# A hybrid decoder trunk: x, p, the vectors and the output pass the host with channels first

## The chip, the cores and the metric

The kernel runs on one core of one Trainium2 chip. The metric is the device time of one execution in microseconds (us).

## The reference

Two residual layers over 2048 tokens of 1024 channels, then a final norm, all in fp32. Cut to what matters:

```python
h = x
for i in range(2):
    hn = rmsnorm(h, norm_gain[i])        # h * rsqrt(mean(h*h over channels) + 1e-6) * gain
    if i == 0:                            # z = hn @ w_in, split in 8
        h = h + concat(retention(q, k, v) * silu(g), stick_breaking(q, k, v) * silu(g)) @ w_out
    else:                                 # RWKV-7 time mixing: six shifted mixes of hn, delta-rule recurrence
        h = h + (y * silu(g)) @ w_out
    gate = sigmoid(h @ ple_gate[i])
    h = h + gate * (p[i] @ ple_proj[i])   # p[i]: 2048 x 256
return rmsnorm(h, final_gain)
```

Every projection by weights takes its input with channels on the 128 partitions, since TensorE contracts over the partitions.

## The kernel before, in words

The tokens go in two halves of 1024 (`w` = 0 and 1), each half in two blocks of 512 (`TB`) or eight tiles of 128. Channels stand in 8 blocks of 128 (`NB`). An fp32 operand is kept as a high and a low fp32r part (`split`: a cast on ACT, a subtraction on DVE or POOL), and a product takes three matmuls (`mm3`, L258 to L260).

Stages, with their place in the profiled span:

- 0 to 300 us: `l0_norm(0)` and `retention(0)`. Eight tiles of x (128 tokens x 1024 channels) are loaded; Square with a sum on ACT gives their 1/rms; PE transposes each 128x128 block (`xp`, L419) into channels first. The result is written to `xT` in DRAM for the residual, and multiplied by gain and 1/rms (`hf`) and split into the activations `hn`. 1/rms is a column for each token tile; four matmuls of a broadcast column by the identity turn it into a row on all partitions (`rbp`, L390). The retention projects one head at a time.
- 300 to 530 us: `stick(0)`, the projections of the stick-breaking heads (each result split again and written to DRAM) and its attention.
- 530 to 740 us: `tail(0, 0)`: out projection, residual (`r`, L798, L799), gate, and the projection of p. p is loaded by tokens and transposed on PE (`pt`, L817). A generator, `next_stats(1)`, runs beside it: it transposes the second half of x (`nt`, L449), writes it to DRAM (`xnext`, L454) and computes its 1/rms.
- 740 to 1210 us: `l1_proj(0)`, the projections of layer 1.
- 1210 to 1910 us: the second half's `l0_norm_next`, `retention(1)` and `stick(1)`. Beside the stick-breaking attention layer 1's recurrence of the first half begins at 1714 us.
- 1910 to 2380 us: that recurrence beside `tail_lean`, which is the second half's tail of layer 0.
- 2380 to 2930 us: `l1_proj(1)`. 2930 to 3610 us: the second half's recurrence beside `tail_lean` of layer 1 for the first half and for block 0 of the second. `tail_lean` transposes p too (`pt`, L996).
- 3610 to 3786 us: `tail(1, 1)` for the last block, and beside it `finish`, which loads the other three blocks' results channels first (`fx`), transposes them on PE (`ft`, L911), scales them by 1/rms on ACT and writes them out by tokens. The last block's own results (32 blocks of 128x128) are transposed at L874, kept, and scaled when its 1/rms is there (L887, L889).

The Tile framework orders the instructions of each engine by its own schedule. DMAs issued on SP run in that order, and one that waits holds back those behind it.

Of the kernel before, what the change touches and what calls it, by code (L numbers as in the profile page):

```python
# [133 lines left out]
class Trunk:  # L134
    def __init__(self, ctx, tc, ins, out):
# [23 lines left out]
        self.rs_kept = self.cst.tile([P, NHALF * NTT], F32, name="rs_kept")  # L159
        self.dd, self.parts = {}, {}  # L160
# [17 lines left out]
    def load_vectors(self):  # L178
        nc, i = self.nc, self.i
        flat = lambda a: a.rearrange("(b p) -> b p", p=P)  # L180
        rows = [
            (V_G0, i["norm_gain"].rearrange("j (b p) -> (j b) p", p=P)),
            (V_GF, flat(i["final_gain"])),
            (V_W0, flat(i["rwkv_w0"][0])),
            (V_A0, flat(i["rwkv_a0"][0])),
            (V_KK, flat(i["rwkv_k_k"][0])),
            (V_KA, flat(i["rwkv_k_a"][0])),
            (V_RK, i["rwkv_r_k"][0].rearrange("(b h) n -> b (h n)", h=2)),
            (V_MU, i["odd_mu"][0].rearrange("j (b p) -> (j b) p", p=P)),
            (V_GN, flat(i["ret_gn_gain"][0])),  # L190
        ]
        n = V_N * NB
        v = self.cst.tile([P, n], F32, name="vec")
        with self.tc.tile_pool(name="vl", bufs=1) as vl, self.tc.tile_pool(name="vps", bufs=1, space=PSUM) as vps:
            t = vl.tile([n, P], F32, name="vrows")
            nc.gpsimd.memset(t, 0.0)
            for j, src in rows:
                nc.sync.dma_start(t[j * NB : j * NB + src.shape[0], :], src)
            yield
            ps = vps.tile([P, n], F32, name="vt")  # L200
            nc.tensor.transpose(ps, t, self.ident[:n, :n])
            nc.vector.tensor_copy(v, ps)
# [162 lines left out]
    def l0_norm(self, w):  # L365
        nc, tc = self.nc, self.tc
        self.hn = self.new_acts()
        self.xT = [self.dr.tile([P, HT], F32, name=self.u("xT")) for _ in range(NB)]
        with (
            tc.tile_pool(name="n0x", bufs=2, side="right") as sx,  # L370
            tc.tile_pool(name="n0", bufs=2, side="right") as sb,
            tc.tile_pool(name="n0p", bufs=1, space=PSUM, side="right") as psp,
        ):
            xs, st = [], sx.tile([P, NTT], F32, name="st", bufs=1)

            def load(t):
                xt = sx.tile([P, D], F32, tag="x", name=self.u("x"), bufs=NTT)
                r0 = w * HT + t * P
                nc.sync.dma_start(xt, self.i["x"][0, r0 : r0 + P, :])
                xs.append(xt)  # L380

            def stats(t):
                sq = sx.tile([P, D], BF16, tag="sq", name=self.u("sq"), bufs=1)
                nc.scalar.activation(sq, xs[t], AF.Square, accum_out=st[:, t : t + 1])

            def scales(tb):
                rs = self.rsqrt(sx, st[:, tb * 4 : tb * 4 + 4], 1.0 / D, RMS_EPS, 4, "rs")
                rbp = psp.tile([P, TB], F32, tag="rb", name=self.u("rbp"))
                for j in range(4):
                    nc.tensor.matmul(  # L390
                        rbp[:, j * P : (j + 1) * P],
                        rs[:, j : j + 1].to_broadcast([P, P]),
                        self.ident,
                        start=True,
                        stop=True,
                    )
                rb = sb.tile([P, TB], F32, tag="rbs", name=self.u("rb"))
                nc.scalar.copy(rb, rbp)
                return rb

            for t in range(4):
                load(t)
            if w == 0:
                vectors = self.load_vectors()
                next(vectors)
            for t in range(4):
                load(t + 4)
                stats(t)
            if w == 0:
                for _ in vectors:  # L410
                    pass
            for tb in range(NTB):
                rb = scales(tb)
                for d in range(NB):
                    if tb == 0 and d % 2:
                        stats(4 + d // 2)
                    xp = psp.tile([P, TB], F32, tag="xp", name=self.u("xp"), bufs=3)
                    for j in range(4):
                        nc.tensor.transpose(xp[:, j * P : (j + 1) * P], xs[tb * 4 + j][:, d * P : (d + 1) * P], self.ident)  # L419
                    xo = sb.tile([P, TB], F32, tag="xo", name=self.u("xo"))  # L420
                    nc.scalar.copy(xo, xp)
                    nc.sync.dma_start(self.xT[d][:, tb * TB : (tb + 1) * TB], xo)
                    hf = sb.tile([P, TB], F32, tag="hf", name=self.u("hf"))
                    nc.vector.scalar_tensor_tensor(hf, xp, self.col(V_G0, d), rb, op0=ALU.mult, op1=ALU.mult)
                    sl = slice(tb * TB, (tb + 1) * TB)
                    self.split(hf, self.hn[d][0][:, sl], self.hn[d][1][:, sl], nc.gpsimd if d % 2 else nc.vector)

    def next_stats(self, w, sb, pt):

        nc = self.nc  # L430
        self.xnext = self.dr.tile([P, NB, HT], F32, name=self.u("xT"))
        st = self.rs_kept.rearrange("p (q t) -> p q t", q=2)
        units, xs = [(t, q) for t in range(NTT) for q in range(2)], []

        def load(t, q):
            x = sb.tile([P, 4, P], F32, tag="nx", name=self.u("nx"))
            r0 = w * HT + t * P
            nc.sync.dma_start(x.rearrange("p a b -> p (a b)"), self.i["x"][0, r0 : r0 + P, q * TB : (q + 1) * TB])
            xs.append(x)

        load(*units[0])
        for n, (t, q) in enumerate(units):
            if n + 1 < len(units):
                load(*units[n + 1])
            yield
            x = xs.pop(0)
            tp = pt.tile([P, 4, P], F32, tag="pt", name=self.u("nt"))
            for j in range(4):
                nc.tensor.transpose(tp[:, j], x[:, j], self.ident)  # L449
# [1441 lines left out]
```

## Time and profile before

| what | value |
|---|---|
| three runs | 3775.52, 3779.46, 3786.1 us; median 3779.46 us |
| profiled execution, its own time | 3787.24 us |
| its span | 3785.5 us |
| mean granted TensorE clock | 0.943 of full speed |
| busy share of the span | PE 93%, DVE 52%, ACT 37%, POOL 26% |

The span runs from the first to the last instruction of the profiled execution; its own time is that execution's as the runs' times are taken. PE is matmul on TensorE, PEld its weight loads, DVE VectorE, ACT ScalarE, POOL GpSimd, SP the engine that issues most DMAs.

### The profile page before, as it was taken

What the parts mean: (1) busy time and instruction counts of PE and PEld (TensorE: products, weight loads), DVE (VectorE), ACT (ScalarE), POOL (GpSimd) and SP (SyncE); (2) the same over time, 40 slices, a digit from 0 to 9 for tenths busy, and PEclk for the clock granted to TensorE, in tenths of its full rate; (3) what the DMA queues carried; (4) which work ended last, traced back from release to release, by engine and by line L of the source; (5) the groups of instructions that cost most, each with busy time, mean ns of one, the idle gap of its engine ahead of it and who ended that gap; (6) DMA issues with size and microseconds to landing.
All of it is one profiled execution on the core that took longest, in us unless ns stands there. A gap on an engine that the chain in (4) does not pass through costs nothing.

```text
span 3785.5 us, 66193 instructions
## 1 busy us (share of the span) xinstructions
PE 3536.1 (93%) x25929; PEld 2801.1 (74%) x25929; DVE 1954.3 (52%) x3884; ACT 1412.1 (37%) x2767; POOL 986.2 (26%) x1036
## 2 busy tenths in 40 slices
PE   8999999899999999998979999899988799999978
PEld 6888877777666788887767777677656677777757
DVE  4334541453675433457956756542574477567532
ACT  5233453344553221445522322243553233223233
POOL 4345543400000222455512312200000143122322
PEclk9999999999999999999969999599989799989989
DMA  6348866655587225546456665343575876556485
GB/s 234 103 170 268 226 191 208 208 168 177 194 260 272 74 95 171 174 107 134 88 150 203 177 179 150 110 143 123 185 240 179 203 226 200 156 166 197 161 284 179
DMA packets 593792, 675.14 MB, mean 178 GB/s; under 512 B 215764, under 2 KB 443976, under 8 KB 562504
## 3 DMA queue, kind: packets, MB, share of 16 engines
q1 hardware_dynamic: 510056, 577.95, 49.3%
q10 hardware_dynamic: 42848, 59.39, 4.4%
q0 software_dynamic: 40576, 33.56, 4.2%
q8 instruction: 205, 3.36, 0.4%
q14 instruction: 107, 0.88, 0.1%
HBM read 414.78 MB, written 255.98 MB: 177 GB/s over the span
## 4 chain that ended last, share of the span: by engine, by line
PE 32%; DMA 8%; DVE 7%; SPq 3%; ACT 1%; issue 1%; POOL 1%; ACTq 0%; POOLq 0%; DVEq 0%
PE pj L258 6%; PE pj L259 6%; PE pj L260 6%; PE g L1490 2%; PE y L1652 2%; PE s L1630 1%; PE y L1649 1%; DMA wraw<-in_odd_w_out 1%; DMA w<-parts 1%; PE u L1593 1%; DMA g<-g 1%; DVE prd L1521 1%; PE x L1615 1%; PE kt L1603 1%; DVE wb L1527 1%
## 5 line engine op out<-in xcount | busy, mean ns | idle before, releaser
L258 PE MATMUL pj<-act,w 128*128 128x512 f32 x1216 | 498.5, 414 | 20.3 <-ACT act L218 9.8
L260 PE MATMUL pj<-act,w 128*128 128x512 f32 x1216 | 498.2, 410 | 4.0 <-POOL w L219 4.0
L259 PE MATMUL pj<-act,w 128*128 128x512 f32 x1216 | 496.6, 409 | 0.4 <-POOL act L219 0.4
L258 PE MATMUL pj<-xs,w 128*128 128x512 f32 x768 | 298.4, 403 | 18.1 <-DMA w<-parts 6.5
L259 PE MATMUL pj<-xs,w 128*128 128x512 f32 x768 | 307.0, 400 | 5.2 <-DVE xs L219 5.1
L260 PE MATMUL pj<-xs,w 128*128 128x512 f32 x768 | 302.4, 397 | 0.0
L258 PEld LDWEIGHTS pj<-act,w 128*128 128x128 f32 x1216 | 237.8, 196 | 72.0 <-ACT act L218 11.3
L260 PEld LDWEIGHTS pj<-act,w 128*128 128x128 f32 x1216 | 237.7, 195 | 56.4 <-POOL w L219 4.9
L259 PEld LDWEIGHTS pj<-act,w 128*128 128x128 f32 x1216 | 238.5, 196 | 50.5 <-POOL act L219 0.8
L258 PE MATMUL pj<-w,act 128*128 128x512 f32 x640 | 259.0, 408 | 10.8 <-ACT sg L535 7.1
L712 DVE TENSOR_TENSOR_SCAN rr<-om,rr,ones 128x512 f32<-128x512 f32 (+3 forms) x160 | 216.7, 1361 | 77.1 <-ACT om L706 68.6
L259 PE MATMUL pj<-w,act 128*128 128x512 f32 x640 | 254.9, 398 | 0.0
L260 PE MATMUL pj<-w,act 128*128 128x512 f32 x640 | 253.5, 399 | 0.0
L721 POOL TENSOR_TENSOR be<-be,rr 128x512 f32<-128x512 f32 (+3 forms) x160 | 167.3, 1048 | 192.6 <-DVE rr L712 87.2
L219 POOL TENSOR_TENSOR w<-wraw,w 128x1024 fp32r<-128x1024 f32 x72 | 159.4, 2218 | 173.4 <-ACT w L218 152.1
L258 PEld LDWEIGHTS pj<-xs,w 128*128 128x128 f32 x768 | 146.9, 192 | 67.2 <-issue 15.6
L1490 PE MATMUL g<-xr,kb 64*128 64x128 f32 x1024 | 149.7, 309 | 34.9 <-DVE grb L1498 20.6
L259 PEld LDWEIGHTS pj<-xs,w 128*128 128x128 f32 x768 | 146.9, 191 | 43.5 <-DVE xs L219 11.8
L260 PEld LDWEIGHTS pj<-xs,w 128*128 128x128 f32 x768 | 147.0, 192 | 34.3 <-issue 3.3
L1490 PEld LDWEIGHTS g<-xr,kb 64*128 64x128 f32 x1024 | 121.6, 203 | 60.0 <-DVE grb L1498 22.2
L258 PEld LDWEIGHTS pj<-w,act 128*128 128x128 f32 x640 | 121.9, 191 | 39.2 <-ACT sg L535 10.3
L218 ACT CAST w<-wraw 128x1024 fp32r<-128x1024 f32 x105 | 104.4, 1000 | 123.0 <-PE pj L260 27.2
(364 smaller groups left out, 7760.2 us busy)
## 6 DMA issues: line engine op xcount, KB each, us to landing
w<-parts SPq DMA_DIRECT2D x145, 1024.0 KB
parts<-w SPq DMA_DIRECT2D x97, 1024.0 KB
wraw<-in_odd_w_in SPq DMA_DIRECT2D x32, 512.0 KB
ar<-ar SPq DMA_DIRECT2D x32, 512.0 KB
w<-v SPq DMA_DIRECT2D x128, 128.0 KB
xr<-ar SPq DMA_DIRECT2D x64, 256.0 KB
kb<-kb SPq DMA_DIRECT2D x32, 512.0 KB
kg<-dk POOLq DMA_DIRECT2D x24, 512.0 KB, 5.0
```

The costliest lines, as they stand in the source:

```text
L218: nc.scalar.copy(hi, src)
L219: (lo_eng or nc.vector).tensor_tensor(lo, src, hi.bitcast(F32), op=ALU.subtract)
L258: nc.tensor.matmul(ps, a[0], b[0], start=first, stop=False)
L259: nc.tensor.matmul(ps, a[0], b[1], start=False, stop=False)
L260: nc.tensor.matmul(ps, a[1], b[0], start=False, stop=last)
L712: nc.vector.tensor_tensor_scan(rr[:, 0:kw][:, ::-1], om[:, ::-1], self.ones.to_broadcast([P, kw]), rr[:, kw : kw + 1], op0=ALU.mult, op1=A ...
L721: nc.gpsimd.tensor_tensor(be, be, rr[:, 1 : kw + 1], op=ALU.mult)
L1490: nc.tensor.matmul(ps[:, j], kb[br, 4 * g + j], xr[br, par, 4 * g + j], start=True, stop=True)
L1521: nc.vector.tensor_tensor(pr[:, :k, :n], nb[:, m, k:].unsqueeze(1).to_broadcast([P, k, n]), wb[:, :k, m:k].to_broadcast([P, k, n]), op=ALU ...
L1527: nc.vector.tensor_tensor(wb[:, :k, k:], wb[:, :k, k:], pr[:, :k, :n], op=ALU.add)
L1593: nc.tensor.matmul(ps[hs, ob], lhs[hs, ob], rhs[hs, ob], start=True, stop=True)
L1652: nc.tensor.matmul(o, d["grb"][hs, ob], uv[hs, par, ob], start=False, stop=True)
```

## The change

The host hands over x twice, as it was and transposed (`xT`, 1024 x 2048), p transposed (`pT`) and all vectors as one table (`vec`); the kernel's output is 1024 x 2048, and the host transposes it. What follows inside:

- `l0_norm`, `next_stats` and `l0_norm_next` are gone. `l0_in` loads 128x512 blocks of `xT` and multiplies them by the gain alone: the high part on ACT, the low part in one operation on DVE. These loads stand between the loads of the first head's weights.
- `l0_stats` loads x by tokens as well, two tiles at a time, and takes its squares. 1/rms stays as columns (`rs0`) and as rows in DRAM (`rb0`). It is applied to the results: in the retention as the scale of the operations that read PSUM, in the stick-breaking projections through one new DVE multiplication for each result, into a tile `f` that has one buffer (the gate's result is written to DRAM straight from it), and for `v` in the operations of its split.
- The tails load p by `pT`. In `finish` and at the end of `tail`, results are multiplied by 1/rms as rows on DVE and written channels first; the end's eight writes go to SP and ACT by turns.

The diff, cut to its core:

```diff
+    def l0_in(self, w, sb, tb, ds):
+
+        nc = self.nc
+        sl = slice(tb * TB, (tb + 1) * TB)
+        for d in ds:
+            x = sb.tile([P, TB], F32, tag="x", name=self.u("x"), bufs=8)
+            nc.sync.dma_start(x, self.xT[d][:, sl])
+            hi, lo = [a[:, sl] for a in self.hn[d]]
+            g = self.col(V_G0, d)
+            nc.scalar.activation(hi, x, AF.Copy, scale=g)
+            nc.vector.scalar_tensor_tensor(lo, x, g, hi.bitcast(F32), op0=ALU.mult, op1=ALU.subtract)
+
+    def l0_stats(self, w, sb, psp):
+
+        nc = self.nc
+        self.rb0 = self.dr.tile([P, HT], F32, name=self.u("rb0"))
+        st = sb.tile([P, NTT], F32, name=self.u("st"), tag="st", bufs=1)
+        for tb in range(NTB):
+            for t in range(4 * tb, 4 * tb + 4):
+                xt = sb.tile([P, D], F32, tag="xt", name=self.u("xt"))
...
+                sq = sb.tile([P, D], BF16, tag="sq", name=self.u("sq"), bufs=1)
+                nc.scalar.activation(sq, xt, AF.Square, accum_out=st[:, t : t + 1])
+            ts = slice(tb * 4, tb * 4 + 4)
+            rs = self.rsqrt(sb, st[:, ts], 1.0 / D, RMS_EPS, 4, "rs")
+            nc.vector.tensor_copy(self.rs0[:, ts], rs)
+            rbp = psp.tile([P, 4, P], F32, tag="tp", name=self.u("rbp"))
...
+                nc.tensor.matmul(rbp[:, j], rs[:, j : j + 1].to_broadcast([P, P]), self.ident, start=True, stop=True)
+            rb = sb.tile([P, TB], F32, tag="rbs", name=self.u("rb"), bufs=1)
+            nc.scalar.copy(rb, rbp.rearrange("p a b -> p (a b)"))
+            nc.sync.dma_start(self.rb0[:, tb * TB : (tb + 1) * TB], rb)
...
                 for b0 in range(0, NB, 2):
+                    if h == 0:
+                        self.l0_in(w, sx, 0, (b0, b0 + 1))
...
+                if h:
+                    return res
+                nc.sync.dma_start(rope, self.i["c_rope"][w * HT : (w + 1) * HT, :].rearrange("(t p) c -> p t c", p=P))
+                self.l0_in(w, sx, 1, range(0, NB))
+                self.l0_stats(w, sx, pq)
...
+                    rs = self.rs0[:, t : t + 1]
+                    nc.scalar.activation(qk[:, 0], ps[:, 0:128], AF.Copy, scale=qks[:, t, h : h + 1])
+                    nc.scalar.activation(qk[:, 1], ps[:, 128:256], AF.Copy, scale=qks[:, t, RH + h : RH + h + 1])
                     v = sb.tile([P, P], F32, tag="v", name=self.u("v"))
-                    nc.vector.tensor_copy(v, ps[:, 256:384])
-                    nc.scalar.activation(sg[:, t], ps[:, 384:512], AF.Silu)
+                    nc.vector.tensor_scalar_mul(v, ps[:, 256:384], rs)
+                    nc.scalar.activation(sg[:, t], ps[:, 384:512], AF.Silu, scale=rs)
...
+                    rs = self.rs0[:, t : t + 1]
+                    nc.scalar.activation(vt[:, 0], ps, AF.Copy, scale=rs)
+                    nc.vector.scalar_tensor_tensor(
+                        vt[:, 1], ps, rs, vt[:, 0].bitcast(F32), op0=ALU.mult, op1=ALU.subtract
+                    )
...
+                        f = sb.tile([P, TB], F32, tag="pf", name=self.u("pf"), bufs=1)
+                        nc.vector.tensor_tensor(f, ps, rbs[t], op=ALU.mult)
+                        if nm == "g":
+                            nc.scalar.dma_start(dst[0, :, sl], f)
+                            return
```

```diff
+                    nc.sync.dma_start(pr, i["pT"][l, d * P : (d + 1) * P, t0_ : t0_ + TB])
+                    self.split(pr, pT[d][0][:, tok(q)], pT[d][1][:, tok(q)])
...
             rs = self.token_rstd(sb, pt, tts=tts)
...
+            for t in ts:
+                rbp = self.rows_of(rs[:, (t - ts[0]) * 4 : (t - ts[0]) * 4 + 4], pt)
+                for ob in range(NB):
+                    o = sb.tile([P, TB], F32, tag="fo", name=self.u("fo"), bufs=8)
+                    nc.vector.tensor_tensor(o, rbp, h1[ob][:, tok(t)], op=ALU.mult)
+                    (nc.scalar if ob % 2 else nc.sync).dma_start(self.out_at(w, ob, t), o)
...
+        rbp = pool.tile([P, TB], F32, tag="pt", name=self.u("rbp"))
+        for j in range(4):
+            self.nc.tensor.matmul(
+                rbp[:, j * P : (j + 1) * P], rs[:, j : j + 1].to_broadcast([P, P]), self.ident, start=True, stop=True
+            )
...
-        def load(t, q):
-            x = sb.tile([P, 4, P], F32, tag="fx", name=self.u("fx"), bufs=3)
-            nc.sync.dma_start(x, h[:, 4 * q : 4 * q + 4, t * P : (t + 1) * P])
+        def load(t, ob):
+            x = sb.tile([P, TB], F32, tag="fx", name=self.u("fx"), bufs=3)
+            nc.sync.dma_start(x, h[:, ob, t * TB : (t + 1) * TB])
...
+        units = [(t, ob) for t in ts for ob in range(NB)]
...
-            x = xs.pop(0)
-            tp = pt.tile([P, 4, P], F32, tag="pt", name=self.u("ft"))
-            for j in range(4):
-                nc.tensor.transpose(tp[:, j], x[:, j], self.ident)
+            if ob == 0:
+                rbp = self.rows_of(rs[:, t * 4 : t * 4 + 4], pt)
             o = sb.tile([P, TB], F32, tag="o", name=self.u("fo"))
-            nc.scalar.activation(o, tp.rearrange("p a b -> p (a b)"), AF.Copy, scale=rs[:, t : t + 1])
-            r0 = w * HT + t * P
-            nc.sync.dma_start(self.out[0, r0 : r0 + P, q * TB : (q + 1) * TB], o)
+            nc.vector.tensor_tensor(o, rbp, xs.pop(0), op=ALU.mult)
+            nc.sync.dma_start(self.out_at(w, ob, t), o)
             yield
```

Where the instructions stand, in rows of the program order (a line number, the operation, output<-inputs, shape; the change has other line numbers).

PE at its start, before: `xp` is a transposed block of x, `pj` the accumulator of a retention projection, `rbp` 1/rms as rows.

```order
L419 MATMUL xp_272<-k,x_118 128x128
L419 MATMUL xp_272<-k,x_120 128x128
L419 MATMUL xp_272<-k,x_122 128x128
L419 MATMUL xp_272<-k,x_124 128x128
L258 MATMUL pj_475<-w_439,act_84 128x512
L258 MATMUL pj_476<-w_439,act_84 128x512
L258 MATMUL pj_538<-w_439,act_84 128x512
L258 MATMUL pj_539<-w_439,act_84 128x512
L390 MATMUL rbp_314<-k,rs_299 128x128 x4
```

The change, its first rows and those around the first `rbp` (here with the numbers of the tiles' turns):

```order
L238 MATMUL pj_318<-w_139,act_93 128x512
L238 MATMUL pj_319<-w_139,act_93 128x512
L238 MATMUL pj_381<-w_139,act_93 128x512
L238 MATMUL pj_382<-w_139,act_93 128x512
L239 MATMUL pj_318<-w_139,act_93 128x512
```

```order
L239 MATMUL pj_88_382<-w_37_187,act_15_107 128x512
L240 MATMUL pj_88_382<-w_37_187,act_16_108 128x512
L374 MATMUL rbp_61_263<-k_60,rs_59_247 128x128 x4
L238 MATMUL pj_102_476<-w_22_139,act_1_93 128x512
L239 MATMUL pj_102_476<-w_22_139,act_1_93 128x512
```

The 64 transposes are gone, the first 96 projection matmuls stand ahead of everything, and the first `rbp` stands behind them, ahead of the next token tiles' projection `pj_102`; `rbp_74`, the second, stands 48 projection matmuls later.

SP near its start, before: `x` are token tiles of 128x1024, `wraw` the first head's weights, `xT` the write of a transposed block.

```order
L379 DMA x_144<-in_x 128x1024
L379 DMA x_148<-in_x 128x1024
L379 DMA x_152<-in_x 128x1024
L379 DMA x_156<-in_x 128x1024
L233 DMA wraw_440<-in_even_w_in 128x4x128
L500 DMA rope_435<-in_c_rope 128x8x192
L422 DMA xT_100<-xo_199 128x512
L422 DMA xT_101<-xo_213 128x512
L233 DMA wraw_440<-in_even_w_in 128x4x128
L233 DMA wraw_448<-in_even_w_in 128x4x128 x2
```

The change: `x` are now 128x512 blocks of `xT`, `xt` the token tiles for the squares, `parts` the write of split weights for the second half.

```order
L351 DMA x_196<-in_xT 128x512
L351 DMA x_200<-in_xT 128x512
L351 DMA x_204<-in_xT 128x512
L351 DMA x_208<-in_xT 128x512
L220 DMA parts_145<-w_139 128x2048
L213 DMA wraw_172<-in_even_w_in 128x4x128 x2
L366 DMA xt_230<-in_x 128x1024
L351 DMA x_212<-in_xT 128x512
L366 DMA xt_234<-in_x 128x1024
L220 DMA parts_161<-w_155 128x2048
L213 DMA wraw_188<-in_even_w_in 128x4x128 x2
L351 DMA x_216<-in_xT 128x512
```

The token tiles have moved from the front to behind all 8 blocks of `xT` of the first 512 tokens, three pairs of weights, `rope` and a write of 1 MB, and they alternate with the rest.

DVE in the first half's stick-breaking attention, before: `rr` is the running sum of a unit, `wT` the low part of transposed attention weights; the gate's projection is read from PSUM by ACT, so it has no row here.

```order
L712 SCALAR_TENSOR_TENSOR rr_4503<-om_4502,rr_4503,ones 128x256
L712 SCALAR_TENSOR_TENSOR rr_4524<-om_4523,rr_4524,ones 128x384
L219 TENSOR_TENSOR wT_4556<-tp_4557,wT_4555 128x128
L712 SCALAR_TENSOR_TENSOR rr_4543<-om_4542,rr_4543,ones 128x512
L219 TENSOR_TENSOR wT_4556<-tp_4567,wT_4555 128x2x128
L712 SCALAR_TENSOR_TENSOR rr_4602<-om_4601,rr_4602,ones 128x128
```

The change: the two `pf` are the two blocks of a gate projection times 1/rms, both in the one buffer `f`.

```order
L635 SCALAR_TENSOR_TENSOR rr_4354<-om_4353,rr_4354,ones 128x128
L635 SCALAR_TENSOR_TENSOR rr_4383<-om_4382,rr_4383,ones 128x256
L551 TENSOR_TENSOR pf_4507<-pj_4368,rb_2359 128x512
L551 TENSOR_TENSOR pf_4510<-pj_4369,rb_2361 128x512
L635 SCALAR_TENSOR_TENSOR rr_4404<-om_4403,rr_4404,ones 128x384
L635 SCALAR_TENSOR_TENSOR rr_4423<-om_4422,rr_4423,ones 128x512
L199 TENSOR_TENSOR wT_4436<-tp_4437,wT_4435 128x128
```

Two multiplications have come into the row of the attention's operations. The second stands right behind the first, and may only write once the DMA that empties the buffer is done.

## Rows read from the trace of the kernel before

**Rows 1.** Groups of lines, PE: count, busy us, mean ns, idle before, its releasers.

```profile
L911 PE MATMUL ft<-k,fx 128*128 128x128 f32 x96 | 18.4, 333 | 15.9 <-DMA fx<-h 14.0 <-ACT fo L913 1.9
L419 PE MATMUL xp<-k,x 128*128 128x128 f32 x64 | 12.4, 341 | 12.6 <-DMA x<-in_x 7.3 <-DVE hf L424 3.6 <-DVE rs L360 1.6
L449 PE MATMUL nt<-k,nx 128*128 128x128 f32 x64 | 9.6, 272 | 0.0
L996 PE MATMUL pt<-k,pr 128*128 128x128 f32 x40 | 8.6, 327 | 1.0 <-PE btp L1409 0.6 <-DMA pr<-in_p 0.4
L817 PE MATMUL pt<-k,pr 128*128 128x128 f32 x24 | 4.2, 276 | 1.1 <-DMA pr<-in_p 1.1
```

**Rows 2.** Windows of stages: us, busy (instructions) of PE, PEld, DVE, ACT, POOL, PEclk, DMA share, GB/s.

```profile
300.00:530.00 230.00, 227.57 (x1227) 194.84 (x1226) 117.17 (x138) 105.51 (x217) 125.75 (x160) 0.99 0.79 229
530.00:740.00 210.00, 201.16 (x900) 163.60 (x899) 55.31 (x80) 73.62 (x134) 93.74 (x66) 0.97 0.65 206
...
1500.00:1910.00 410.00, 377.86 (x2697) 323.47 (x2696) 261.26 (x355) 195.44 (x418) 206.74 (x292) 0.97 0.51 128
```

**Rows 3.** Timeline of PE at the start: start us, us, line, operands, count.

```profile
40.98 1.04 PE L419 MATMUL xp<-k,x 128*128 128x128 f32 x8
...
71.67 0.50 PE L258 MATMUL pj<-w,act 128*128 128x512 f32 x1
```

**Rows 4.** Windows of line L911 alone: us, PE, PEld, PEclk, DMA share, GB/s.

```profile
3653.00:3770.00 117.00, 8.20 (x56) 6.94 (x56) 0.98 0.69 233
```

**Rows 5.** Waits of PE, 530 to 740 us: us in all, count, longest.

```profile
PE pj L258 <- DVE r L799: 4.6, 1, 4.6
PE pj L258 <- ACT act L218: 4.2, 1, 4.2
```

**Rows 6.** Timeline around the first of these waits (in brackets idle time before, its releaser).

```profile
567.24 4.02 SPq L798 DMA_DIRECT2D r<-xT  x2
573.21 0.37 ACTq L454 DMA_DIRECT2D xT<-no  x1
576.78 1.41 DVE L799 TENSOR_TENSOR r<-pj,r 128x512 f32<-128x512 f32 x2 [19.06 <-DMA r<-xT]
```

**Rows 7.** Windows at the start, columns as in rows 2.

```profile
0.00:66.00 66.00, 47.63 (x215) 38.56 (x216) 29.98 (x60) 39.02 (x69) 27.80 (x26) 1.00 0.82 280
50.00:55.00 5.00, 5.00 (x25) 4.18 (x24) 4.63 (x8) 4.66 (x11) 4.66 (x4) 1.00 1.06 379
65.00:80.00 15.00, 14.68 (x74) 11.95 (x73) 3.98 (x14) 4.66 (x13) 3.30 (x6) 1.00 0.00 0
```

**Rows 8.** Group of lines, ACT: the squares of x.

```profile
L384 ACT ACTIVATE sq<-x 128x1024 bf16<-128x1024 f32 x8 | 8.5, 1056 | 5.5 <-DMA x<-in_x 5.4
```

**Rows 9.** Timeline of the end: DVE and SP's queue.

```profile
3769.89 0.69 DVE L849 TENSOR_TENSOR o<-o,g 128x512 f32<-128x512 f32 x1
...
3774.43 0.16 DVE L354 TENSOR_SCALAR rs<-ssp 128x4 f32<-128x4 f32 x1
...
3776.80 1.67 DVE L889 TENSOR_SCALAR fo<-fo,rs 128x512 f32<-128x512 f32 x4
3777.32 4.46 SPq L891 DMA_DIRECT2D out<-fo  x8
```

**Rows 10.** DMA issues, 300 to 530 us: count, KB each, median us to landing.

```profile
q<-dq POOLq DMA_DIRECT2D x16, 256.0 KB, 5.1
```

**Rows 11.** Timeline in the first stick-breaking stage: weights `wT`, and PE's use of them.

```profile
400.51 1.12 DVE L219 TENSOR_TENSOR wT<-tp,wT 128x384 fp32r<-128x384 f32 x2
...
404.79 0.28 PE L258 MATMUL ot<-wT,vg 128*128 128x256 f32 x1
```

**Rows 12.** Waits of PE, 1495 to 1910 us, columns as in rows 5.

```profile
PE ot L259 <- DVE wT L219: 8.5, 9, 3.0
```

**Rows 13.** The page's DMA line: packets, bytes and mean rate over the span.

```profile
DMA packets 593792, 675.14 MB, mean 178 GB/s; under 512 B 215764, under 2 KB 443976, under 8 KB 562504
```

**Rows 14.** A window in the last stage, columns as in rows 2.

```profile
3630.00:3640.00 10.00, 2.31 (x9) 1.60 (x10) 3.43 (x15) 2.00 (x3) 1.75 (x2) 0.50 1.01 308
```

More of the change, by code (lines that the diff above doesn't have):

```diff
@@ L178, in load_vectors @@
     def load_vectors(self):
[L179 to L202, printed above, removed]
+        nc = self.nc
+        v = self.cst.tile([P, V_N * NB], F32, name="vec")
+        nc.scalar.dma_start(v, self.i["vec"])
         self.vec = v
@@ L401, in l0_norm @@
[L401 to L426, printed above, removed]
@@ L607, in stick @@
             sb = pool("sk", 2, side="right")
+            rbs = []
+            for t in range(NTB):
+                rbs.append(sb.tile([P, TB], F32, tag=f"rb{t}", name=self.u("rb"), bufs=1))
+                nc.sync.dma_start(rbs[t], self.rb0[:, t * TB : (t + 1) * TB])
             def vproj():
@@ L867, in tail @@
                     next(side, None)
-                if l and ob % 4 == 3:
-                    ft.append([])
-                    for k, t in enumerate(tts):
-                        tp = pt.tile([P, 4, P], F32, tag="pt", name=self.u("ft"))
-                        for j in range(4):
-                            nc.tensor.transpose(tp[:, j], h1[ob - 3 + j][:, t * P - t0 : (t + 1) * P - t0], self.ident)
-                        o = sb.tile([P, TB], F32, tag="fo", name=self.u("fo"), bufs=8)
-                        (nc.vector.tensor_copy if k % 2 else nc.scalar.copy)(o, tp.rearrange("p a b -> p (a b)"))
-                        ft[-1].append(o)
             for _ in side:
@@ L993, in block @@
                 if ob < 2:
-                    tp = pp.tile([P, 4, P], F32, tag="pp", name=self.u("pt"))
-                    for j in range(4):
-                        nc.tensor.transpose(tp[:, j], pr[:, j], self.ident)
                     x = tuple(sb.tile([P, TB], F32R, tag=f"pT{ob}{j}", name=self.u("pT")) for j in range(2))
-                    self.split(tp.rearrange("p a b -> p (a b)"), x[0], x[1])
+                    self.split(pr, x[0], x[1])
                     pT.append(x)
@@ L1774, in run @@
                 self.mixed = {}
-                self.l0_norm_next() if w else self.l0_norm(w)
+                self.hn = self.new_acts()
+                self.xT = [self.i["xT"][d * P : (d + 1) * P, w * HT : (w + 1) * HT] for d in range(NB)]
                 with self.tc.tile_pool(name="skj", bufs=3, space=PSUM) as pj:
-                    for _ in self.retention(w, pj):
-                        pass
+                    with self.tc.tile_pool(name="n0", bufs=2, side="right") as sx:
+                        for _ in self.retention(w, pj, sx):
+                            pass
                     self.stick(w, pj)
                 if w == 0:
-                    h1 = self.tail(0, w, mixed, sb_gate, self.xT, lambda sb, pt: self.next_stats(w + 1, sb, pt))
+                    h1 = self.tail(0, w, mixed, sb_gate, self.xT)
                     dg = self.l1_proj(w, h1)
@@ L1810, in side @@
             def side(sb, pt):
[L1811 to L1812 removed]
+                yield from self.finish(w - 1, h2[0], self.rs_kept, range(NTB), sb, pt)
+                yield from self.finish(w, h2[1], self.rs_kept[:, NTT:], range(1), sb, pt)
             self.tail(1, w, mB, gB, h1, side, [1])
```

176 lines of the change are left out of this document (51 added, 125 removed).

## The prediction

> **What bounds the kernel.** I read the page first, then the windows of the stages, the waits of PE in each stage, and the timeline where a stage waits. PE is busy in nearly all of the span: 227.6 of 230 us in the first half's stick-breaking stage and 201.2 of 210 us in its tail, at 0.99 and 0.97 of the full clock, while DVE and ACT have half their time free [rows 2]. So a PE instruction that goes is worth its place in PE's queue where PE runs without a gap, and nothing where PE was waiting anyway. The same rows show where PE is weakest: with the recurrence beside the attention, 1500 to 1910 us, it is busy 377.9 of 410 us, and DVE 261.3.
>
> **Transposes taken away.** By the groups, 64 `xp`, 64 `nt`, 96 `ft` from `fx`, 40 and 24 `pt` go [rows 1], and the 32 `ft` of the last block, which the diff shows. Which of them stood on the path?
>
> The 64 `xp` run in the first 66 us, where DMA sets the pace (start, below): 0. Of the 96 `ft`, 56 run behind 3653 us [rows 4]; the other 40 stand where line L911 had nearly all its waits, 14.0 us for the load `fx` [rows 1], so PE waits there with or without them: 0. Of the 32 last ones, the first 16 run among projections and the other 16 behind the last projection (those I count with the end). On the path are then: in the first tail 64 `nt` and 16 of the `pt` of L817, 80; in `tail_lean` 40; in the last stage 56, 16 and the other 8 of L817, 80. Together 200. The idle time ahead of them is 0.0 for `nt` and about 1 us for either `pt` [rows 1], so PE had no free time there.
>
> What is one worth? The mean duration is 272 ns [rows 1], but PE overlaps them: eight lasted 1.04 us together [rows 3], so less the last one's 0.27 us there are 0.77 us for seven steps, 0.11 us each. 200 x 0.11 = **22 us gained**. The bounds are 0.11 and 0.272 us each.
>
> The Trainium skill ("TensorE: Matmul & The Clock Gate", Part 4: PE-mode transpose) gives about 275 ns for a transpose within a kernel. The mean duration in the groups, 272 ns, agrees with it, but the eight in 1.04 us do not if it is taken as the cost of each; by 275 ns the 200 would give 55 us.
>
> **Waits of PE in the first tail.** Two waits stand there, 4.6 us for the residual sum on DVE and 4.2 us for a cast on ACT [rows 5]. The first is a load: DVE had been idle 19.06 us when `r` came from `xT`, issued at 567.24 us, while the writes of `no` (transposed x, in 512-byte pieces) went out beside it [rows 6]. These 16 writes of 256 KB go, 4.2 MB, and ACT loses the side work's 32 operations, a square and a copy for each. Bounds 0 and 8.8; both lose their neighbour, but the load still stands in SP's row: **6 us gained**.
>
> **Row sums of 1/rms added.** The end and `finish` get 16 matmuls of a broadcast column, two passes each; 8 of them stand in the dense part: 16 x 0.11 = **1.8 us lost**. The others stand in waits or in the end's sum.
>
> **The end.** Before, 14.9 us pass from the last sum `o` (ends 3770.58) to the span's end, 3785.5. The squares' sum is read at 3774.43, after the 16 last transposes; 1/rms is there at 3776.80, 2.4 us later; the writes are issued one after another on SP for 4.46 us, until 3781.78, and 3.7 us later all is over [rows 9]. After: the transposes go, so the sum comes at about 3773.0 and 1/rms at 3775.4; the row takes about 1.5; then eight DVE multiplications of 0.69 us each, as L849's [rows 9], 5.5 us, to 3782.4; an issue 0.6 and the landing 3.7: 3786.7. **1.2 us lost**.
>
> **The start.** The first 96 projection matmuls no longer wait for any transposition, but the next ones, and above all those behind the second `rbp`, wait for 1/rms of the first half's 8 token tiles. On SP ahead of the eighth tile's landing stand, by the order and the shapes: constants 0.3 MB, 16 blocks of x 4.2, seven pairs of weights 3.7, `rope` 0.8, five writes of split weights 5.2, the 8 tiles 4.2, small ones 0.3; 18.7 MB. Before, the first 66 us moved 280 GB/s, or 18.5 MB, and then nothing for 15 us [rows 7]: the same volume, now read instead of partly written. Behind the landing come a square 1.06 us [rows 8] with its sum, 1/rms 2.4 (as at the end), the row 1, and PE's small matmuls 2.8: 7.4 us. PE's 145th projection matmul began at 71.67 us [rows 3]. At 280 GB/s it would begin at 66.8 + 7.4 = 74.2, a loss of 2.5; at 379 GB/s, the best window of 5 us [rows 7], at 56.7, a gain of 15. I take 300 GB/s, near the mean, since nothing waits for PE's transposes between the loads now: 69.7, **2 us gained**. Bounds -3 and 15, were the queue never held up.
>
> **DVE in the stick-breaking stages.** Each half gets 24 multiplications of 0.69 us, 16.6 us, 33 in all. In the first half DVE has 113 us free and PE 2.4 [rows 2], so their volume is hidden there. The wait is another matter: `f` has one buffer, and the gate's two blocks come one behind the other (the order above), so the second waits until the write of the first has landed, and all attention sums queue behind it on DVE. No write's landing is shown; the nearest row is a load of the same 256 KB, 5.1 us from issue to landing [rows 10]. How much DVE's delay may be before PE waits: `wT` done at 401.63, used by PE at 404.79 [rows 11], 3.2 us. So a pair costs up to 5.1 + 0.7 - 3.2 = 2.6 us, and there are 8 gate projections in both halves: 0 to 21 us. For the volume, only the second half matters: PE idles 32 of 410 us there, 8.5 of them for DVE's `wT` [rows 2, 12]; if those waits grow in step with DVE's load by half, 4 us. I take a quarter of the first bound, 5 us, since before the change PE hardly waited for DVE in spite of DVE's own idle stretches, and 1 for the second: **6 us lost**.
>
> Nothing: ACT's saved copies and casts (ACT is busy half of the time or less in each stage), `pf` for q and k, whose readers are quick, and the loads of x for the squares in the second half, which take the place of `xnext`'s loads and lie in `l1_proj(0)`.
>
> **Sum.** 22 + 6 - 1.8 - 1.2 + 2 - 6 = 21 us gained. The profiled execution's own time, 3787.2, becomes 3766; it lies 7.8 us above the median of the runs, 3779.5, which becomes **3758 us**. What a measurement can tell from no change is about 0.3%, 11.3 us: below 3768.1 is faster, above 3790.8 slower.
>
> **Rivals.**
> - *The sums as forecast* (0.54), 3758, with a range of its own from 3748 to 3768.
> - *The first loads run at their best rate* (0.10): the start gains 10 instead of 2 (18.7 MB at 344 GB/s), so 3750. For it: 379 GB/s was reached. Against it: the split and its writes stand between.
> - *DVE eats it* (0.25): every gate pair costs its 2.6 us and the second half's waits grow by 2, 23 us lost instead of 6: 4 us gained, 3775.5, no measurable change. For it: the order puts the second `pf` next to the first in the rows shown, and DVE waits in its queue. Against it: PE has the other projections to run.
> - *The wait for 1/rms* (0.08), the slower one. If the first 18.7 MB move only at the span's mean rate, 178 GB/s [rows 13], because many different transfers alternate in one queue, they take 105.1 us, and the 145th matmul begins at 112.5: 40.8 us lost, PE with nothing else to do. 19 (the sum without the start) - 40.8 = -21.8, so 3801. It decides from a loss of 30.3 us at the start on, which is 198 GB/s. Against it: the first 66 us of before had 280.
> - *Every transpose costs its whole duration* (0.03): 200 x 0.272 = 54.4 instead of 22 gives 53.4 in all, 3726. Against it: the eight in 1.04 us.
>
> PE waiting long for a DMA costs more than the wait: from 3630 to 3640 us, PE busy 2.3 of 10, its granted clock was 0.50, the lower level of 1.2 GHz [rows 14]. The Trainium skill ("TensorE: Matmul & The Clock Gate", Part 1, HAM oscillation) says that waits for DMA between bursts of matmuls bring the clock down again and again; that speaks against this change at its start, where PE now waits for the x tiles; there the trace of before granted 1.00 throughout [rows 7], so no run here shows it at this place.
>
> **How the numbers follow.** The forecast is the first case. Its bounds with the second case's reach down to 3741, a little less with the tail's full 8.8 us: I take 3737. Upward the third case's 3775.5 and some us of a poorer start: 3783. Left out are the fourth and fifth cases and the ends of the others, about 0.2. Faster holds the first two cases nearly whole, the fifth and a sixth of the third: 0.65. Same: the rest of the third and the upper end of the first: 0.24. Slower: the fourth and the worst of the third: 0.11.
>
> **What would show it.** In the first tail, no wait of 4 us for `r` and 201 us of PE work become some 192. In the last stage, no `ft`; the tail end from the last `o` takes 16 us. At the start, the matmul behind the second `rbp` begins near 70 us; beyond 100 the fourth case is true. In the stick-breaking stages, DVE's waits of `pf` on the DMA of `pf` are there, 3 to 6 us each, and PE's waits for `wT` tell what they cost. Wrong I would be above all if PE's waits for DVE grow by more than 20 us, or if another order moves waits that no row shows.

## The result, and the profile after

The change takes 3759.91 us (median of 7 runs, 3751.43 to 3770.94) against 3783.07 us (7 runs) of the kernel before on the same chip: ratio 0.994, 95% interval 0.9921 to 0.9958. On a second chip it was 3758.64 against 3775.72 us, 0.9952 (0.9935 to 0.997). The profiled execution took 3754.9 us with a span of 3752.8, 32.7 us less than the span before; about 9 us of that are scatter, since the one profile lay above its kernel's median and the other below.

The top of the page of the change, which answers to the table of before:

```profile
span 3752.8 us, 65409 instructions
...
PE 3492.1 (93%) x25640; PEld 2764.9 (74%) x25640; DVE 1973.5 (53%) x3959; ACT 1375.9 (37%) x2671; POOL 974.1 (26%) x1019
```

The shares have hardly moved, so the page alone says nothing of where the time went. Places that both programs pass do. Start times of PE's instructions in both traces, in us (`ot`, `z`, `g` and `y` are products of the attention and of the recurrence, `ssp` a tail's sum of squares):

| place | before | change | difference |
|---|---|---|---|
| 145th projection matmul of the retention | 71.67 | 65.22 | -6.5 |
| last `ot`, first half's attention | 526.8 | 519.6 | -7.2 |
| `ssp`, first tail | 742.9 | 711.6 | -31.3 |
| last retention product, second half | 1482.2 | 1446.1 | -36.1 |
| first `z`, second half | 1528.2 | 1482.3 | -45.9 |
| last `ot`, second half | 1904.5 | 1857.9 | -46.6 |
| last `y`, first recurrence | 2456.2 | 2418.3 | -37.9 |
| first `g`, second recurrence | 2940.3 | 2905.6 | -34.7 |
| last `y`, second recurrence | 3612.3 | 3583.8 | -28.5 |
| end | 3785.5 | 3752.8 | -32.7 |

Until 1905 us the change is ahead by more than forecast; beside the two recurrences it loses 15 us again. The step from the second half's last retention product to its first `z` holds 17 projection matmuls fewer in the change (155 for 172), so it is read over a longer stretch below.

The waits of PE in its first tail, the answer to [rows 5]:

```profile
PE pj L238 <- DVE r L722: 3.2, 2, 1.6
```

And the windows there, PEclk third from the right; the same stretch of before follows:

```profile
519.60:602.80 83.20, 79.89 (x352) 65.25 (x351) 25.98 (x31) 25.83 (x42) 40.31 (x27) 1.00 0.65 205
```

```profile
535.00:540.00 5.00, 0.76 (x3) 0.50 (x2) 1.94 (x4) 1.82 (x3) 0.00 (x0) 0.83 0.93 333
540.00:545.00 5.00, 5.00 (x13) 3.88 (x12) 3.46 (x3) 3.10 (x7) 4.52 (x3) 0.50 0.74 246
545.00:550.00 5.00, 5.00 (x24) 4.00 (x24) 2.09 (x4) 2.34 (x6) 0.00 (x0) 0.98 0.35 112
...
578.00:583.00 5.00, 5.00 (x13) 3.84 (x13) 0.19 (x1) 1.47 (x4) 2.54 (x2) 0.53 1.01 370
```

PE is "busy" all the time from 540 to 545 us, and does 13 matmuls instead of 24: behind each of the two long waits stood some 5 us at 0.50, the lower level of 1.2 GHz. In the change the waits are 1.6 us long, and the clock stays at 1.00.

The end, timeline of the change, the answer to [rows 9]:

```profile
3735.29 0.69 DVE L768 TENSOR_TENSOR o<-o,g 128x512 f32<-128x512 f32 x1
...
3737.49 1.75 PE L990 MATMUL ssp<-ones,ssacc 128*128 128x1 f32 x8 [3.10 <-DVE ssacc L774]
...
3741.67 2.08 PE L806 MATMUL rbp<-k,rs 128*128 128x128 f32 x8 [2.43 <-DVE rs L341]
3743.79 4.88 DVE L796 TENSOR_TENSOR fo<-rbp,h 128x512 f32<-128x512 f32 x8 [2.17 <-PE rbp L806]
3744.51 3.92 SPq L797 DMA_DIRECT2D out<-fo  x4
3745.11 3.93 ACTq L797 DMA_DIRECT2D out<-fo  x4
```

From the last `o` to the end 16.8 us pass, forecast 16.1, before 14.9.

### The profile page after: what moved, and what is told of

It is laid out like the page before. It is cut to its first block, busy times and chain, and to the rows that moved or that the text cites. A ratio compares the mean times of both kernels' runs of the same rounds, so it can differ in the third digit from the quotient of the medians.

```text
span 3752.8 us, 65409 instructions
## 1 busy us (share of the span) xinstructions
PE 3492.1 (93%) x25640; PEld 2764.9 (74%) x25640; DVE 1973.5 (53%) x3959; ACT 1375.9 (37%) x2671; POOL 974.1 (26%) x1019
## 5 line engine op out<-in xcount | busy, mean ns | idle before, releaser
L238 PE MATMUL pj<-act,w 128*128 128x512 f32 x1216 | 493.4, 410 | 26.0 <-ACT act L198 12.3
L239 PE MATMUL pj<-act,w 128*128 128x512 f32 x1216 | 492.5, 405 | 2.9 <-DVE act L199 2.1
L240 PE MATMUL pj<-act,w 128*128 128x512 f32 x1216 | 491.1, 405 | 3.6 <-POOL w L199 3.6
L238 PE MATMUL pj<-xs,w 128*128 128x512 f32 x768 | 297.7, 401 | 22.3 <-ACT xs L198 9.7
L238 PEld LDWEIGHTS pj<-act,w 128*128 128x128 f32 x1216 | 234.4, 193 | 81.6 <-ACT act L198 14.9
L240 PEld LDWEIGHTS pj<-act,w 128*128 128x128 f32 x1216 | 234.5, 193 | 54.3 <-POOL w L199 4.8
L239 PEld LDWEIGHTS pj<-act,w 128*128 128x128 f32 x1216 | 234.8, 193 | 53.6 <-DVE act L199 3.6
L635 DVE TENSOR_TENSOR_SCAN rr<-om,rr,ones 128x512 f32<-128x512 f32 (+3 forms) x160 | 200.4, 1266 | 46.8 <-ACT om L629 39.1
L644 POOL TENSOR_TENSOR be<-be,rr 128x512 f32<-128x512 f32 (+3 forms) x160 | 178.1, 1115 | 167.1 <-DVE rr L635 90.6
L1399 PE MATMUL g<-xr,kb 64*128 64x128 f32 x1024 | 147.7, 307 | 32.5 <-DVE grb L1407 18.7
L238 PEld LDWEIGHTS pj<-w,act 128*128 128x128 f32 x640 | 121.7, 191 | 50.7 <-ACT sg L447 14.9
```

What stands on the lines that cost most here:

```text
L238: nc.tensor.matmul(ps, a[0], b[0], start=first, stop=False)
L239: nc.tensor.matmul(ps, a[0], b[1], start=False, stop=False)
L240: nc.tensor.matmul(ps, a[1], b[0], start=False, stop=last)
L635: nc.vector.tensor_tensor_scan(rr[:, 0:kw][:, ::-1], om[:, ::-1], self.ones.to_broadcast([P, kw]), rr[:, kw : kw + 1], op0=ALU.mult, op1=A ...
L644: nc.gpsimd.tensor_tensor(be, be, rr[:, 1 : kw + 1], op=ALU.mult)
L1399: nc.tensor.matmul(ps[:, j], kb[br, 4 * g + j], xr[br, par, 4 * g + j], start=True, stop=True)
```

## The experiments

All ran beside the kernel before on their chip; the chips differ, so small differences are read from the ratios. "Beside tail_lean" is from the second half's last `ot` to the first recurrence's last `y`, "second recurrence" from its first `g` to its last `y`, "last" from there to the end, each of one profiled execution. That execution lay up to 15 us off its kernel's median: x4's 15 below it, that of outputs only 13 above, those of gate in two buffers and of the change again 10 to 11 above. "Second recurrence" and "last" also hold different work from kernel to kernel: 397 to 443 projection matmuls stand behind the last `y`.

| kernel | median us | ratio (95%) | first tail | beside tail_lean | second recurrence | last |
|---|---|---|---|---|---|---|
| before | 3775.7 to 3783.1 | 1 | 216.1 | 551.7 | 672.0 | 173.2 |
| change | 3759.9 | 0.994 (0.992 to 0.996) | 192.0 | 560.4 | 678.2 | 169.0 |
| change again | 3758.6 | 0.995 (0.994 to 0.997) | 191.8 | 565.3 | 690.1 | 169.3 |
| layer 0 only | 3730.9 | 0.988 (0.984 to 0.992) | 194.0 | 539.8 | 664.0 | 174.7 |
| outputs only | 3783.6 | 1.002 (1.000 to 1.004) | 211.7 | 560.0 | 676.4 | 173.6 |
| transposes back | 3762.4 | 0.996 (0.995 to 0.998) | 201.4 | 567.5 | 684.3 | 170.2 |
| traffic back | 3776.7 | 1.000 (0.998 to 1.002) | 204.9 | 555.0 | 685.4 | 172.2 |
| tail_lean, transposes x4 | 3748.1 | 0.992 (0.989 to 0.995) | 191.6 | 551.2 | 666.6 | 173.6 |
| tail_lean, transposes x1 | 3730.3 | 0.988 (0.984 to 0.992) | 191.7 | 543.4 | 672.4 | 172.9 |
| tail_lean, p by tokens | 3731.7 | 0.989 (0.985 to 0.993) | 191.4 | 546.0 | 666.9 | 171.0 |
| slower pace | 3752.1 | 0.994 (0.991 to 0.996) | 191.4 | 558.1 | 686.0 | 166.3 |
| squares first | 3729.9 | 0.987 (0.984 to 0.991) | 191.7 | 543.2 | 672.2 | 172.5 |
| gate in two buffers | 3743.0 | 0.991 (0.988 to 0.993) | 194.0 | 538.8 | 685.6 | 166.9 |
| squares first, p by tokens | 3733.9 | 0.989 (0.987 to 0.992) | 191.7 | 539.4 | 676.0 | 174.3 |

**The two halves of the change.** Layer 0 only takes `tail`, `finish`, `tail_lean` and the host's side of p and the output from the kernel before; outputs only takes layer 0 from the kernel before, and the outputs and p from the change.

> The layer-0 part alone: x and the vectors pass as in the change, p is loaded by tokens and transposed on PE again, and the output is transposed on PE and written by tokens as before. Theory: most of the gain is in the first tail, which no longer writes the transposed x; the p and output parts give only what the last stage and the end showed (6.7 us gained, 2.5 lost) and 16 transposes of p in the first tail (1.5), while the 40 of tail_lean are absorbed by the recurrence. So 5 to 7 us slower than the whole change (about 3766), and the first tail 193 to 195 us long. Rival: the gain comes from the outputs, then this stands within 5 us of the kernel before (3778 or more).

> The other part alone: p and the output pass with channels first, x and layer 0 are as before. Theory: layer 0 stays as before (retention's end near 297 us, the first tail 214 us, less the 16 transposes of p), the last stage and the end take 168 to 170 us instead of 173, and the second recurrence, whose rows in PE's order are the same as in the run with the squares first, takes 672 us as there: 5 to 10 us faster than before in the parts that it touches, and the rest by the order of the first recurrence. Rival: the part itself slows the recurrences; then the second takes 678 to 685 us.

My theory missed the first by 35 us: layer 0 alone is not 5 us worse than the change but 23 to 29 us better. The outputs alone give nothing that can be measured, where 5 to 10 us were expected; their last part took 173.6 us and not 168 to 170, but it holds 429 projection matmuls and the change's 402. The second recurrence, 676.4 us, fell between theory and rival. The first tail came as expected in both (194.0; 211.7 with some 212.5 expected).

**The first tail taken apart.**

```diff
+    def only_pe(self, sb, pt):          # transposes back
+        for n in range(2 * NTT):
+            yield
+            tp = pt.tile([P, 4, P], F32, tag="pt", name=self.u("nt"))
+            for j in range(4):
+                self.nc.tensor.transpose(tp[:, j], self.ident, self.ident)
```

```diff
+            yield                       # traffic back, for each loaded 128x512 of x
+            nc.scalar.activation(o, x, AF.Square, accum_out=st[:, q, t : t + 1])
...
+            nc.scalar.copy(o, x)
+            nc.scalar.dma_start(xnext[:, 4 * q : 4 * q + 4, t * P : (t + 1) * P], o)
```

> The change with 64 transposes of a resident tile put back beside the first tail, at the places where they stood, without their loads, ACT work and writes. Theory: a transpose costs 0.09 to 0.11 us of PE's queue and opens no gap: the first tail goes from 191.9 to about 198.5 us, the granted clock there stays 1.00, the whole 6 to 7 us slower. Rival 1: each costs its whole duration, 0.272 us: 209 us. Rival 2: they are what made the gaps: gaps of 4 us and stretches at 0.50 come back.

> The change with the other half of that side work put back: 16 loads of x, a square and a copy on ACT for each, and 16 writes in 512-byte pieces to a DRAM tensor that nobody reads; no transposes. Theory: the load r is late behind these writes again, PE has gaps of 4 us or more in the first 60 us of the tail, and the clock falls to 0.50 behind them: 203 to 208 us instead of 191.9, the whole 11 to 16 us slower. Rival: the gaps came from the other order of the program; then the tail stays within 195 us.

The transposes cost 9.4 us, the traffic (loads, ACT's work and writes together) 12.9, in all 22.3 of the 24.1 that the change saved here. Which of the three parts of the traffic does it was not tried. Its tail came as expected, the whole 17 to 18 us slower than the change instead of 11 to 16. PE's waits for the residual (us in all, count, longest) are

```profile
PE pj L238 <- DVE r L722: 14.2, 4, 10.2
```

The tail with the transposes missed by 3 us, and neither rival's number came; the whole was 2 to 4 us slower than the change and not 6 to 7. 63 of the 64 transposes took 6.05 us from start to start, 0.096 each. Ten times the projection matmul right behind a group of them took 0.31 us to the next one's start instead of 0.23, 0.9 us in all. The rest, 2.7 us, is the clock: six transposes stood ahead of a gap, and the matmuls behind it came slowly. The timeline of PE shows both.

```profile
528.59 0.82 PE L804 MATMUL nt<-k 128*128 128x128 f32 x6
532.87 0.77 PE L238 MATMUL pj<-act,w 128*128 128x512 f32 x1 [3.46 <-ACT act L198]
533.43 0.63 PE L239 MATMUL pj<-act,w 128*128 128x512 f32 x1
...
538.49 0.82 PE L804 MATMUL nt<-k 128*128 128x128 f32 x6
539.06 0.48 PE L238 MATMUL pj<-act,w 128*128 128x512 f32 x1
539.38 0.39 PE L239 MATMUL pj<-act,w 128*128 128x512 f32 x1
539.61 0.39 PE L240 MATMUL pj<-act,w 128*128 128x512 f32 x1
```

The change's two waits of 1.6 us became one of 3.5, and behind it 13 matmuls came 0.43 us apart instead of 0.23.

**What the 40 transposes in tail_lean were worth.** Either four (x1) or 16 (x4) transposes of a resident tile for each block of p, or `tail_lean` whole from before, or the pace constants of the merges a tenth higher:

```diff
+                    tp = pp.tile([P, 4, P], F32, tag="pp", name=self.u("pt"))
+                    for j in range(4):
+                        nc.tensor.transpose(tp[:, j], self.ident, self.ident)
```

```diff
-RATIO = 1.0
+RATIO = 1.1
...
-RATIO_B = 0.95
+RATIO_B = 1.05
```

> The change with four times the removed transposes of p put back in tail_lean, of a resident tile: 64 beside the first half's recurrence, 96 beside the second half's. Theory: the recurrence's own chain sets the end of both stages; PE's extra 7 and 10 us fall into its waits, and from the first g to the last y each recurrence stays within 3 us of the change's 717 and 679 us. Rival: PE is the bound there, since it is busy 95%: 7 and 10 us more, 17 in all.

> The change, with tail_lean alone as before: there p comes by tokens and is transposed on PE (40 transposes). Theory: taking those transposes out is what made both recurrences longer in the change than in the layer-0 part alone (717 against 688 us and 678 against 664 us); with them back the recurrences take 690 to 705 and 664 to 670 us, the last stage and the end stay at the change's 169 us, and the whole comes to 3720 to 3735 us. Rival: the longer recurrences come from the output part or from p in the tails; then this stays at 3755 to 3765 us.

> The change with the removed number of transposes (40, of a resident tile) put back in tail_lean, a fourth of the run with four times as many, which took 704 and 667 us for the recurrences. Theory: what helps is that a PE instruction stands there, in the order and in PE's queue: 705 or less and 672 or less here too, about 3745 us. Rival 1: what helps is the amount of PE work, which holds the clock: then a fourth of it gives at most half, 711 and 675 or more. Rival 2: the runs differ by chance: 717 and 680 again.

> The change with the pace constants of the two merges raised by a tenth (RATIO 1.0 to 1.1, RATIO_B 0.95 to 1.05), so that tail_lean's work is laid out more slowly beside the recurrence. Theory of balance: in the change tail_lean's first part ends 92 us before the recurrence, which then runs alone at a granted clock of 0.50; with a slower pace that stretch shrinks to 75 us or less and the first recurrence to 705 us or less. Rival: the pace is not the cause; the stretch may shrink, but the recurrence stays at 710 us or more, since its own chain is what is long.

From its first `g` to its last `y` the first recurrence took 717.0 us in the change (717.8 before), 703.8 with x4, 704.1 with p by tokens, 697.9 with x1 and 709.2 with the slower pace. With more PE work the kernel got no slower: 23 to 30 us faster with x1 and p by tokens, 8 to 12 with x4, whose interval overlaps the change's. So those transposes did not cost 0.1 us each there. For x4 neither number came; for p by tokens and x1 the theories' stages came (x1's whole was 15 us faster than its theory said), but "a PE instruction standing there helps" is no explanation yet, as the next runs showed. The slower pace shrank the stretch that the recurrence runs alone (from the tail's last `ssp`) from 92 to 75.5 us and left the stage long; its 709.2 us miss the theory's 705 and lie at the rival's 710.

**The same work in another row.** Squares first only moves loads of x and their squares at the start of each half's layer 0 (the first 60 us, and around 1100 to 1200 us); gate in two buffers only exchanges a buffer.

```diff
+                self.l0_stats(w, sx, pq, [0])
                 self.l0_in(w, sx, 1, range(0, NB))
-                self.l0_stats(w, sx, pq)
+                self.l0_stats(w, sx, pq, [1])
```

```diff
+                        if nm == "g":
+                            f = sb.tile([P, 2, TB], F32R, tag="pst", name=self.u("pst"))[:, 0].bitcast(F32)
```

> The change with the first four token tiles and their 1/rms ahead of the second 512 tokens' blocks of xT. Theory: the bytes ahead of the second 1/rms stay the same and DMA sets the pace there, so the retention's end moves by less than 3 us from 286.7; PE's wait of 6.2 us ahead of the first rbp goes and comes back behind. Rival: the place of the tiles in the queue is what holds PE: 6 us earlier.

> The change with the gate's product in the two-buffered tile of the other products instead of the one buffer f. It does the same work; PE's row in both recurrences comes out in another order. Theory on f: DVE's waits for the gate's writes (5.9 us in all) go, and the first stick-breaking stage stays at 233 us, since PE never waited for them. Rival: the stage gets 2 us or more shorter. Theory on the order: the recurrences may take anything from 688 to 718 and 664 to 686 us, and 717 and 680 would be chance. Rival: 714 to 720 and 676 to 686 again, then not the order but the change's work makes them long.

> The change itself, once more, beside the others on one chip. Theory: PE's row decides: 714 to 720 and 677 to 686 us for the recurrences, as in the change and in the run with the transposes back in the first tail, which has the same rows; 3750 to 3762 us in all, 20 us or more above the run with the squares first. Rival: one execution differs from the next as much as one order from another; then this comes out near 3735.

> Two edits together: the first squares ahead of the second 512 tokens' blocks, and tail_lean with p by tokens and its transposes. Each alone gave 3730 us. Theory: the start's 2 us stays, the rest is drawn from the orders again: 3720 to 3745. Rival: both are gains of their own and add up to 3705.

Squares first gained 2 us at the retention's end (284.7) as expected, and 17 in the stage beside `tail_lean`, over 600 us behind its last edited place, whose code it leaves alone. What it did change is the schedule: PE's row in both recurrences differs from the change's. The change and the change again have the same row in both recurrences, and so has transposes back but for four of the 6497 matmuls of the first stage: 560.4, 565.3 and 567.5 us beside `tail_lean`. Every other row with the new layer 0 took 538.8 to 558.1. Two of these are nearly one row, from two different edits: squares first and gate in two buffers, 543.2 and 538.8 us, have the same last 5531 of 6497 matmuls there. These took 455.2 and 451.3 us, the last 5531 in the three runs of the change's row 468.7 to 475.8. So here the time went with the row and not with the edit (two rows, five executions); and since both of these kernels hold the whole outputs part, that part's work is not what makes the stage long. The windows of that stage, first the change, then squares first:

```profile
1857.90:2418.30 560.40, 513.49 (x6499) 402.24 (x6497) 329.00 (x810) 152.24 (x312) 132.74 (x105) 0.85 0.57 163
```

```profile
1849.10:2392.30 543.20, 499.80 (x6496) 393.05 (x6497) 326.13 (x810) 152.05 (x312) 128.31 (x105) 0.88 0.57 168
```

The same 6500 instructions keep PE "busy" 13.7 us longer at the lower mean clock; its idle time differs by 3.5 us only (46.9 and 43.4). PE's longest waits there (us in all, count, longest), the change and then squares first, stand at other places of the recurrence:

```profile
PE f L1481 <- DVE tds L1472: 11.0, 3, 4.3
PE yt L1595 <- issue: 6.4, 1, 6.4
PE yt L1595 <- DVE tds L1495: 4.2, 1, 4.2
```

```profile
PE y L1560 <- DVE xs L1549: 9.4, 2, 8.3
PE f L1483 <- DVE tds L1474: 6.4, 3, 2.5
```

In the second recurrence equal rows differ more: 678.2, 684.3 and 690.1 us for the change's, 672.0 and 664.0 for before and layer 0 only, which share theirs, 672.2 and 676.4 for squares first and outputs only. There the runs do not separate the row from scatter. The two edits together did not add up.

## Why the prediction came out, point by point

The time was right, 3759.9 for 3758, and by luck: two large errors of its terms cancelled. By the profiles the start gave 7 us (2 forecast) and the first tail 24 (15 forecast); from there to the second half's last `ot` came another 15 that I had at nothing or at a loss, and beside the recurrences and in `l1_proj(1)` 18 were lost that I had at a gain of 4. The end gave 4 (6 forecast).

- **Start**, 2 us: 6.5 measured. The 18.7 MB were there by 57 us, at 328 GB/s on average and not 300, nearer to the second rival's 344, and PE's second `rbp` stood at 60.17 us:

```profile
0.00:26.00 26.00, 14.89 (x53) 11.01 (x53) 12.69 (x16) 14.87 (x22) 8.62 (x11) 1.00 0.97 342
0.00:57.00 57.00, 37.53 (x138) 28.61 (x139) 22.46 (x45) 30.88 (x52) 16.37 (x17) 0.91 0.93 328
26.00:66.00 40.00, 30.74 (x131) 24.17 (x132) 14.05 (x50) 18.65 (x39) 8.72 (x8) 0.87 0.74 260
45.00:50.00 5.00, 3.73 (x12) 2.88 (x12) 2.58 (x6) 4.97 (x14) 2.25 (x3) 0.50 0.95 333
```

```profile
43.92 2.08 PE L374 MATMUL rbp<-k,rs 128*128 128x128 f32 x8 [5.79 <-DVE rs L341]
...
60.17 1.05 PE L374 MATMUL rbp<-k,rs 128*128 128x128 f32 x8
```

  The wait for 1/rms is there (PE 5.8 us for `rs` ahead of the first `rbp`), and small; the clock did fall behind it, to 0.50, as I had feared for this place. The slower rival failed at its rate.
- **Waits of the first tail**, 6 us: mis-sized. Gaps went from 9.5 to 4.0 us from start to start, 5.5 less; but I priced only the waits, not the slow matmuls behind them. Behind the two waits 25 matmuls came 0.43 us apart instead of 0.23, in the change 3: 4.7 us more. Another 22 took 0.31 us right behind a group of transposes, 1.9 us that belong to the next term. The Trainium skill ("TensorE: Matmul & The Clock Gate", Part 1, HAM oscillation) says that waits for DMA between bursts of matmuls bring the clock down again and again; the trace of before agrees here with 0.50 and 0.53 behind the waits, of which one hung on a load and the other on a cast by ACT.
- **Transposes**, 22 us: the price of 0.11 held where they stood in dense work (0.09 to 0.10, and 0.08 for the matmul behind each group). I missed 16 passes of `nr` in the first tail, 1.6 us, which went as well. The step that failed is "on the path", for the 40 in `tail_lean`: put back, they cost nothing. The last stage with the end shrank by 4.2 us, where 8.8 less 1.8 and 1.2 were forecast. Among the kernels with the same 402 projection matmuls behind the last `y` it took 166.3 to 170.2 us with the new outputs (four) and 173.2 and 174.7 with the old, so this part of the sum held.
- **DVE**, 6 us lost: nothing. From the first `z` to the last `ot` of the first half, with the same 516 projection matmuls, PE took 196.9 us before and 196.7 in the change. DVE's waits of `pf` for the write of `dg` are there, as the step said, but five times and 2.2 us at most in the change (two groups: the two stick-breaking stages).

```profile
DVE pf L551 <- DMA dg<-pf: 2.5, 2, 2.2
...
DVE pf L551 <- DMA dg<-pf: 3.3, 3, 2.2
```

  With two buffers they vanish, and the stage from the retention's end is not shorter (236.1 us instead of 232.9, with 18 projection matmuls more in it, some 4 us). 5.1 us for a load was a poor stand-in for a write, whose landing the change's DMA issues show, beside [rows 10] (count, KB each, median us):

```profile
dg<-pf ACTq DMA_DIRECT2D x16, 256.0 KB, 2.1
```

- **Not forecast:** PE's gap ahead of the second half's first `z` (5.8 us before, 7.9 in outputs only) went in every kernel with the new layer 0.

```profile
1528.24 0.45 PE L697 MATMUL z<-kg,q 128*128 128x128 f32 x1 [5.80 <-issue]
```

  From that half's first retention product to its last `ot`, with the same 1392 projection matmuls, the change took 635.5 us instead of 646.1, 10.6 less; the other kernels with the new layer 0 took 626 to 640, outputs only 651.4. The load `q` that `z` needs landed 22 us after its issue before, 9 in the change. On POOL's queue it stood behind six loads of `v` before and ahead of them now; that this order is the cause was only argued. The other 4.7 of the 15 us, from the first tail's `ssp` to that first product, are within the differences between kernels with the new layer 0 (509 to 517 us; 515.5 before).
- **Not forecast, and against it:** the order in the recurrences. Layer 0 only keeps 46 to 50 us; the whole change keeps 17 to 23 of them, the rest is lost in the recurrences' rows as its schedule lays them out.

Left open: which feature of the row makes it slow. The lower clock goes with it, and so do longer waits of `f` for `tds` (10.8 to 13.9 us in the three runs of the change's row, 6.4 and 4.1 in squares first and gate in two buffers); which comes first was not tried.

## What to carry to other kernels

Price a wait of PE with the half-speed matmuls behind it, and a load that lands late with all that it holds up. Where a scheduler lays out two interleaved streams, an edit anywhere can change the row of all that follows: compare the rows, and judge an edit by the stages that it touches, not by the total alone. A small edit that reshuffles the rest, as squares first (3729.9 us, with three others within 2 us of it the fastest here), is worth trying as such.

## What the runs showed of the hardware

One wait of 3.5 us brought the granted clock down where two of 1.6 us close together did not. Six transposes of 0.1 us each ahead of such a wait did not prevent it. A projection matmul right behind a group of transposes took 0.31 us to the next one's start, elsewhere 0.23. And a broadcast row (`rbp`, eight passes) took 2.08 us at the lower clock, at the end and first at the start, and 1.05 us in the start's dense stretch.
